# Selective-scan stage of a hybrid encoder layer on one Trainium2 core: which engine builds the mask G and the skip term, where filler matmuls stand, and where two sets of background weight sums run

## The chip, the cores and the metric

One NeuronCore of a Trainium2 chip runs the whole program. TensorE (PE) multiplies matrices, VectorE (DVE) and ScalarE (ACT) work on rows of up to 128 partitions, GpSimd (POOL) can do the same kind of element-wise work and issues DMAs, SyncE (SP) only issues DMAs. Each engine runs its own instructions strictly in order and waits on semaphores for the others. The metric is the device time of one execution in microseconds (us); lower is better.

## The reference

For 512 tokens of width 2048, in float32:

```python
h = rmsnorm(x, norm_w);  u = h @ w_in                 # z, x/B/C, dt fwd/bwd, q, kv, z_attn, two gates
xbc = silu(dwconv(xbc, conv_w, conv_b))               # x: 32 heads of 64; B, C: 4 groups of 128
y_fwd = ssd_scan(xs, dtf, a_f, bm, cm)                # chunks of 128 tokens
y_bwd = flip(ssd_scan(flip(xs), flip(dtb), a_b, flip(bm), flip(cm)))
y = y_fwd + y_bwd + d_skip[:, None] * xs              # the last term is the skip term
y = rmsnorm per group of (y * silu(z))
o = bidir_attention(...) * silu(z_attn)               # 16 heads, full softmax over 512 tokens
merged = sigmoid(g_ssm) * (y @ w_proj_ssm) + sigmoid(g_attn) * (o @ w_proj_attn)
out = rmsnorm(x + merged @ w_out, final_norm_w)
```

Inside one chunk `ssd_scan` needs, for every head, a 128 by 128 mask: decay(l, s) times (C_l . B_s) times dt_s. The kernel adds the forward mask (l not before s) and the backward one and multiplies by x once. That combined mask is the tile `G` below.

## The kernel before

Every float32 matmul is made of three matmuls of a faster 32-bit type: a weight is split by ACT into a rounded part `wh` (line 163 or 433) and by DVE into the rest `wl` (164 or 434), and PE adds wh\*x_h, wl\*x_h and wh\*x_l (lines 168 to 170, 578 to 580). The stages in order of time in the profile:

- 0 to 40 us: x is loaded, normalised and turned.
- 40 to 567 us: the dt columns, the x/B/C columns of group 0, and the gates z, g_ssm and g_attn by a Strassen scheme.
- 567 to about 1120 us: the scan, four groups of eight heads (`ssd_group`), which the change is about. PE's time is mostly filled with other products: the x/B/C columns of the next group, the q and kv columns, the z_attn columns. They are generators in a queue `fill`. The function `gap()` takes a fixed share of them, so that PE has something to do while the other engines prepare the next step.
- 1190 to about 1500 us: attention, head by head (`scores`, `trans`, `pv`), filled with the q/k/v products of later heads.
- 1500 us to the end: the projections of both branches and the output projection, by the Strassen scheme, whose weight sums T1 and T3 (`t_jobs`) have been formed in DRAM: for each, one DMA copies one weight block and a second DMA adds another to it (`accum_op`). There are 32 such DMAs for `wps` (the SSM projection) and 32 for `wpa` (the attention projection), all on POOL's queue. `wps` has them issued in the scan, one at every second `gap()`; `wpa` has them issued in attention, four per head in heads 0 to 7, each time after a tiny POOL product `pace` (line 1325) that waits for the head's softmax.

One group of the scan has three parts.

1. *Turning.* B and four tiles `xs` of x are turned by PE (line 942, four 128 by 128 transposes each, into the two banks of tag `pb`) and copied out by ACT (`b_h` line 947, `xT` line 953). In group 0, `dt_turn` and `dt_sums` come first: they turn dt and da and make the decay factors.
2. *State.* For three steps and two directions POOL weights x (`xw`, line 989), ACT and DVE split it (992, 993), PE forms the local state `loc`, DVE and ACT update and split the state, PE multiplies it by C (`off`), DVE scales it (1017) and POOL adds it to `yo` (1018). `yo` was set to the skip term by four POOL products per group (line 1022).
3. *Diagonal.* Four chunks c times two halves q of four heads. `cb_make` forms C.B on PE and masks it to `cbf` and `cbb` (DVE, 1043 and 1044). `seg_make` loads `da` (two broadcast DMAs on SP), DVE scans each (1056) and adds them to `E` (1059), ACT takes the exponential (1060), DVE multiplies `cbf` by the forward dt into `G` (1064), POOL multiplies `cbb` by the backward dt (1065), DVE adds (1066) and multiplies by E (1067). One gap later PE uses `G` (`diag`, line 1077); after the second half DVE and ACT gate and normalise y (`y_norm`).

PE's instructions stand in the order in which the code is written. The other engines' order is set by a planner with its own costs, except for the calls in `keep_in_program_order`. The order of the whole program ahead of the scan and behind attention is the same in both kernels.

The gap sizes of a group are set here (before the change):

```python
shares = [0.5 if g else 1.5, 1.1] + [0.8] * 6 + [1.25] * 10
left = [0, (10 * 48, 10 * 48, 9 * 48, 10 * 48)[g] / sum(shares)]
```

A unit of 48 is one product tile: 48 matmuls of 128 by 512.

Of the kernel before, what the change touches and what calls it, by code (L numbers as in the profile page):

```python
# [11 lines left out]
F32 = mybir.dt.float32  # L12
F32R = mybir.dt.float32r
I32 = mybir.dt.int32
AF = mybir.ActivationFunctionType
# [57 lines left out]
def build(tc, a):  # L73
# [231 lines left out]
    def dt_turn():  # L305
        tp = pb()
        dt64 = dt_t[0]
        for c in range(TT):
            pe.transpose(tp[:, c * P:(c + 1) * P], dt64[:, c * P:(c + 1) * P], ident)
        tpv = tp.rearrange("p (c k) -> p c k", c=TT)  # L310
        act.copy(dtT, tpv[:, :, 0:64])
        act.copy(daT, tpv[:, :, 64:128])

    def dt_sums():
        sm = pa()
        smv = sm.rearrange("p (k d c h) -> p k d c h", k=2, d=2, c=TT)
        for kk, dd, mask in ((0, 0, m_le), (0, 1, m_ge), (1, 0, m_gt), (1, 1, m_lt)):
            pe.matmul(smv[:, kk, dd], mask, daT[:, :, dd * NH:(dd + 1) * NH], start=True, stop=True)
        act.activation(ex.rearrange("p k d c h -> p (k d c h)"), sm, AF.Exp)
        tot = pb()  # L320
        pe.matmul(tot[:, 0:256], ones, daT.rearrange("p c h -> p (c h)"), start=True, stop=True)
        act.activation(dec.rearrange("p c h -> p (c h)"), tot[:, 0:256], AF.Exp)
        for dd in range(2):
            dve.tensor_mul(wst[:, dd], ex[:, 1, dd], dtT[:, :, dd * NH:(dd + 1) * NH])
# [152 lines left out]
    def t_jobs(w):  # L477

        jobs = []
        for cp in range(2):  # L480
            for name, kh, cb in (("T1", 0, 0), ("T3", 1, 1)):
                for m in range(4):
                    d = t_d[w, cp, name][:, m * 1024:(m + 1) * 1024]
                    i = 2 * len(jobs) // 2
                    jobs.append((lambda d=d, cp=cp, kh=kh, cb=cb, m=m: pool.dma_start(d, a[w][cp, kh, cb, m]),
                                 lambda d=d, cp=cp, m=m: pool.dma_start(d, a[w][cp, 0, 1, m], accum_op=ALU.add)))
        order = []
        for i in range(len(jobs) + 2):
            if i < len(jobs):
                order.append(jobs[i][0])  # L490
            if i >= 2:
                order.append(jobs[i - 2][1])
        return deque(order)

    background = t_jobs("wps")

    def in_background(n=1):
        for _ in range(n):
            if background:
                tc.keep_in_program_order(background.popleft()())  # L500
# [355 lines left out]
    def bc_heads(t, n):  # L856

        return t.unsqueeze(2).broadcast_to([P, t.shape[1], n])

    def flat(t):  # L860
        return t.rearrange("p h k -> p (h k)")
# [67 lines left out]
    def ssd_group(g):  # L929
# [15 lines left out]
        def post_b():  # L945
            tp = transposed(BT)
            act.copy(flat(b_h), tp)
            dve.tensor_sub(flat(b_l), tp, flat(b_h).bitcast(F32))

        def post_x(ct, xs):  # L950
            def f():
                tp = transposed(xs)
                act.copy(xT[:, :, ct * P:(ct + 1) * P], tp.rearrange("p (c k) -> p c k", c=TT))
            return f
# [6 lines left out]
                fill.add(("xbc", g + 1) if i == 5 else "xbc", xbc_gen(g + 1, i, tmp2))  # L961
        for kind, n in ((("qkv", 4),), (("qkv", 4),), (("qkv", 2), ("za", 1)), (("za", 10),))[g]:
            add_fill(kind, n)
        shares = [0.5 if g else 1.5, 1.1] + [0.8] * 6 + [1.25] * 10
        left = [0, (10 * 48, 10 * 48, 9 * 48, 10 * 48)[g] / sum(shares)]

        def gap():
            if len(shares) % 2:
                in_background()
            left[0] += shares.pop(0) * left[1]  # L970
            left[0] -= fill.run(left[0])

        gap()
        if g == 0:
            dt_turn()
            dt_sums()
        post_b()
        for ct in range(4):
            post_x(ct, xss[ct])()
        gap()  # L980

# [14 lines left out]
        def state(dd, c, xw):  # L996
            loc = pa("loc")
            mm3(loc, b_h[:, c, :], b_l[:, c, :], xw[0], xw[1], True, True)
            if S[dd] is None:
                S[dd] = sw.tile([P, HPG, 64], F32, tag=f"S{dd}", name=f"S{dd}")  # L1000
                dve.tensor_copy(flat(S[dd]), loc)
            else:
                s_ = S[dd]
                dve.tensor_mul(s_, s_, bc_heads(dec[:, c, dd * NH + g * HPG:dd * NH + (g + 1) * HPG], 64))
                dve.tensor_add(flat(s_), flat(s_), loc)
            s_h = sw.tile([P, SEQ], F32R, tag="r", bufs=6, name="s_h")
            s_l = sw.tile([P, SEQ], F32R, tag="r", bufs=6, name="s_l")
            act.copy(s_h, flat(S[dd]))
            dve.tensor_sub(s_l, flat(S[dd]), s_h.bitcast(F32))
            return s_h, s_l  # L1010
# [7 lines left out]
            pool.tensor_add(yo[:, c], yo[:, c], tmp)  # L1018

        nxt = [state_in(0, 0), state_in(1, 3)]  # L1020
        for c in range(TT):
            pool.tensor_mul(yoh[:, c], xTh[:, c], bc_heads(dsk[:, hs], 64))
        for i in range(3):
            ss = [state(0, i, nxt[0]), state(1, 3 - i, nxt[1])]
            if i < 2:
                nxt = [state_in(0, i + 1), state_in(1, 2 - i)]
            gap()
            if turns:
                y_turn(*turns.popleft())
            offdiag(0, i + 1, ss[0])  # L1030
            offdiag(1, 2 - i, ss[1])
            gap()
# [4 lines left out]
        def cb_make(c):  # L1037
# [6 lines left out]
            dve.tensor_mul(cbb, cb[:, 0:P], m_ge)  # L1044
            cbs[c] = (cbf, cbb)

        def seg_make(c, q):

            h0 = g * HPG + q * 4
            sums = []  # L1050
            for dd, mask in ((0, scan_f), (1, scan_b)):
                da = sw.tile([P, 4, P], F32, tag=f"da{dd}", bufs=2, name=f"da{dd}")
                src = da_d[dd * NH + h0:dd * NH + h0 + 4, c * P:(c + 1) * P]
                tc.keep_in_program_order(nc.sync.dma_start(da, src.unsqueeze(0).broadcast_to([P, 4, P])))
                sums.append(tmp2("sum"))
                dve.tensor_tensor_scan(sums[dd], flat(da), mask, 0.0, ALU.add, ALU.mult)  # L1056
            sf, sb = (t.rearrange("p (h l) -> p h l", h=4) for t in sums)
            E = sw.tile([P, 4, P], F32, tag="E", bufs=2, name="E")
            dve.tensor_add(E, sf, sb[:, :, ::-1])
            act.activation(flat(E), flat(E), AF.Exp)  # L1060
            G = sw.tile([P, 4, P], F32, tag="G", bufs=2, name="G")
            G2 = tmp2("G2").rearrange("p (h l) -> p h l", h=4)
            cbf, cbb = cbs[c]
            dve.tensor_mul(G, bc_heads(dtT[:, c, h0:h0 + 4], P), cbf.unsqueeze(1).broadcast_to([P, 4, P]))
            pool.tensor_mul(G2, bc_heads(dtT[:, c, NH + h0:NH + h0 + 4], P), cbb.unsqueeze(1).broadcast_to([P, 4, P]))
            dve.tensor_add(G, G, G2)
            dve.tensor_mul(G, G, E)
            return G

# [13 lines left out]
                turns.append((c, g, y))  # L1083

        last = None
        for c in range(TT):
            cb_make(c)
            for q in range(2):
                G = seg_make(c, q)
                if q == 1:  # L1090
                    zs[c] = z_load(c, g)
                gap()
                if q == 1 and len(turns) > 1:
                    y_turn(*turns.popleft())
                if last:
                    diag(*last)
                last = (c, q, G)
# [202 lines left out]
    fill.run(24)  # L1300

    heads = {}
    in_background(len(background))
    background.extend(t_jobs("wpa"))
    pace = few(1)

    def scores(hd, t):
        qh, ql, kh, kl, stack, zt = qks[hd]
        tk = slice(t * P, (t + 1) * P)
        s = pa("s")  # L1310
        pe.matmul(s, qh[:, tk], kh, start=True, stop=False)
        pe.matmul(s, qh[:, tk], kl, start=False, stop=False)
        pe.matmul(s, ql[:, tk], kh, start=False, stop=False)
        pe.matmul(s, stack[:, tk], kra, start=False, stop=False)
        pe.matmul(s, stack[:, tk], krb, start=False, stop=True)
        mx, nm, sm_ = (hi.tile([P, 1], F32, tag=n, bufs=4, name=n) for n in ("mx", "nm", "sm_"))
        dve.tensor_reduce(mx, s, AX.X, ALU.max)
        dve.tensor_scalar_mul(nm, mx, -SCALE)  # L1318
        pr = at_t("pr")
        act.activation(pr, s, AF.Exp, bias=nm, scale=SCALE, accum_out=sm_)  # L1320
        dve.reciprocal(sm_, sm_)
        dve.tensor_scalar_mul(pr, pr, sm_)
        heads[hd][2][t] = pr
        if background and t == 1:
            pool.tensor_mul(pace, sm_, sm_)
            in_background(4)

    def trans(hd, t):
        tk = slice(t * P, (t + 1) * P)
# [468 lines left out]
```

## Time and profile before

| | |
|---|---|
| median of 3 runs | 2020.08 us (2014.58 to 2021.41) |
| the profiled execution | 2014.14 us, of which the span below is 2012.4 us |
| PE, DVE, ACT, POOL busy over the span | 96%, 76%, 49%, 16% |
| scan stage, 565 to 1120 us: PE, DVE, ACT, POOL busy | 532.6, 462.8, 303.2, 174.2 of 555 us |

A busy PE counts a matmul as 0.39 us long, although in a steady stage a new one starts every 0.225 us (222 in 50 us), so the busy time hides 0.16 us at the start of each wait. The clock column in a table by stage is the share of full TensorE clock that was granted. Waits are named by the engine and line that ended them.

### The profile page before, as it was taken

Reading aid. Unit: us, or ns where it says so; the run is one execution under the profiler, and the core shown is the slowest. Engines: PE = TensorE matmul, PEld = TensorE weight load, DVE = VectorE, ACT = ScalarE, POOL = GpSimd, SP = SyncE. Lnnn points to the kernel's source line nnn. Section 1 sums busy time; section 2 is a strip of 40 time slices with the busy share of each in tenths; the row PEclk is TensorE's granted clock in tenths of the full one; section 3 lists DMA queues with packets and bytes.
Section 4 is the critical chain, followed back from the end, with each engine's and each line's share of the span. In section 5 each row is a group of like instructions: output and inputs, shape, how many; then the busy total and the mean of one; then the engine's idle time right before and its main releaser. Section 6 shows DMA issues by size and latency. Waiting matters only on the chain.

```text
span 2012.4 us, 24716 instructions
## 1 busy us (share of the span) xinstructions
PE 1940.6 (96%) x9026; PEld 1603.2 (80%) x9026; DVE 1520.6 (76%) x2000; ACT 985.2 (49%) x1370; POOL 323.2 (16%) x357
## 2 busy tenths in 40 slices
PE   6999999999999999999999999999999999999997
PEld 4888888888878778777788888887878787888886
DVE  7976676676659979899787577666676899879467
ACT  6444445444444655646546444444455555444343
POOL 0001001001023243152331011110011111100011
PEclk9999999999999999999999999999999999999999
DMA  5468558558446756776675857783278787847446
GB/s 192 162 191 213 147 136 220 146 131 224 127 157 166 222 164 194 243 214 205 182 199 157 240 163 201 204 221 112 75 205 299 221 290 286 286 157 247 158 90 161
DMA packets 168907, 382.78 MB, mean 190 GB/s; under 512 B 16272, under 2 KB 65552, under 8 KB 168592
## 3 DMA queue, kind: packets, MB, share of 16 engines
q1 hardware_dynamic: 103248, 233.61, 35.5%
q0 software_dynamic: 30656, 103.30, 23.5%
q10 hardware_dynamic: 34880, 44.28, 6.1%
q8 instruction: 71, 1.16, 0.2%
q14 instruction: 52, 0.43, 0.1%
HBM read 329.22 MB, written 98.04 MB: 212 GB/s over the span
## 4 chain that ended last, share of the span: by engine, by line
PE 70%; DVE 14%; DMA 7%; issue 5%; ACT 3%; POOL 1%; SPq 0%; DVEq 0%; POOLq 0%; ACTq 0%
PE P L579 11%; PE P L580 11%; PE P L578 11%; PE za L168 2%; PE za L169 2%; PE za L170 2%; DVE sum L1056 2%; PE xbc L168 2%; PE xbc L169 2%; PE xbc L170 2%; DVE wl L164 2%; PE f L1565 1%; PE f L1566 1%; PE f L1567 1%; DMA wraw<-wps 1%
## 5 line engine op out<-in xcount | busy, mean ns | idle before, releaser
L433 ACT CAST wh<-X 128x1024 fp32r<-128x1024 f32 x164 | 172.4, 1054 | 196.4 <-PE P L580 152.1
L434 DVE TENSOR_TENSOR wl<-X,wh 128x1024 fp32r<-128x1024 f32 x164 | 199.9, 1223 | 90.7 <-ACT wh L433 90.3
L164 DVE TENSOR_TENSOR wl<-wraw,wh 128x1024 fp32r<-128x1024 f32 (+2 forms) x148 | 176.6, 1194 | 83.6 <-ACT wh L163 83.1
L163 ACT CAST wh<-wraw 128x1024 fp32r<-128x1024 f32 (+2 forms) x150 | 145.0, 969 | 132.0 <-PE xbc L169 35.5
L434 DVE TENSOR_TENSOR wl<-Y,wh 128x1024 fp32r<-128x1024 f32 x88 | 107.6, 1224 | 70.3 <-ACT wh L433 70.3
L168 PE MATMUL xbc<-h_h,wh 128*128 128x512 f32 x384 | 151.8, 395 | 0.0
L433 ACT CAST wh<-Y 128x1024 fp32r<-128x1024 f32 x88 | 92.7, 1054 | 117.0 <-PE P L580 105.8
L170 PE MATMUL xbc<-h_h,wl 128*128 128x512 f32 x384 | 149.9, 390 | 0.0
L169 PE MATMUL xbc<-h_l,wh 128*128 128x512 f32 x384 | 149.7, 390 | 0.0
L578 PE MATMUL P<-wh,h_h 128*128 128x512 f32 x384 | 149.4, 389 | 0.0
L579 PE MATMUL P<-wl,h_h 128*128 128x512 f32 x384 | 149.4, 389 | 0.0
L580 PE MATMUL P<-wh,h_l 128*128 128x512 f32 x384 | 149.4, 389 | 0.0
L434 DVE TENSOR_TENSOR wl<-wraw,wh 128x1024 fp32r<-128x1024 f32 x68 | 83.2, 1223 | 63.7 <-ACT wh L433 63.7
L433 ACT CAST wh<-wraw 128x1024 fp32r<-128x1024 f32 x68 | 71.6, 1053 | 117.5 <-PE P L580 63.5
L579 PE MATMUL P<-wl,S 128*128 128x512 f32 x288 | 112.4, 390 | 0.5 <-DVE wl L434 0.3
L578 PE MATMUL P<-wh,S 128*128 128x512 f32 x288 | 112.1, 389 | 0.0
L580 PE MATMUL P<-wh,S 128*128 128x512 f32 x288 | 112.1, 389 | 0.0
L168 PE MATMUL za<-h_h,wh 128*128 128x512 f32 x256 | 101.1, 395 | 0.0
L170 PE MATMUL za<-h_h,wl 128*128 128x512 f32 x256 | 99.8, 390 | 0.0
L169 PE MATMUL za<-h_l,wh 128*128 128x512 f32 x256 | 99.6, 389 | 0.0
L1056 DVE TENSOR_TENSOR_SCAN sum<-da,scn 128x512 f32<-128x512 f32 x64 | 86.3, 1362 | 0.0
L1320 ACT ACTIVATE pr<-s,nm 128x512 f32<-128x512 f32 x64 | 44.1, 690 | 83.6 <-DVE nm L1318 82.8
(743 smaller groups left out, 5213.9 us busy)
## 6 DMA issues: line engine op xcount, KB each, us to landing
wraw<-wi SPq DMA_DIRECT2D x102, 512.0 KB, 4.0
T_wps<-wps POOLq DMA_DIRECT2D x32, 512.0 KB, 6.2
da<-da_d SPq DMA_DIRECT2D x64, 256.0 KB, 4.5
T_wpa<-wpa POOLq DMA_DIRECT2D x32, 512.0 KB, 9.5
wraw<-wps SPq DMA_DIRECT2D x24, 512.0 KB, 5.6
wraw<-wo SPq DMA_DIRECT2D x20, 512.0 KB, 3.6
xbc_d<-xbc ACTq DMA_DIRECT2D x24, 256.0 KB, 3.1
wraw<-wun SPq DMA_DIRECT2D x16, 384.0 KB, 3.1
```

What stands on the lines that cost most here:

```text
L163: act.copy(h, raw)
L164: (dve if ahead[0] else pool).tensor_sub(l, raw, h.bitcast(F32))
L168: pe.matmul(out, wh, xh, start=start, stop=False)
L169: pe.matmul(out, wh, xl, start=False, stop=False)
L170: pe.matmul(out, wl, xh, start=False, stop=stop)
L433: i = act.copy(hi_, raw)
L434: dve.tensor_sub(lo_, raw, hi_.bitcast(F32))
L578: pe.matmul(bs[i], xh, wh, start=(j == 0), stop=False)
L579: pe.matmul(bs[i], xh, wl, start=False, stop=False)
L580: pe.matmul(bs[i], xl, wh, start=False, stop=(j == 7))
L1056: dve.tensor_tensor_scan(sums[dd], flat(da), mask, 0.0, ALU.add, ALU.mult)
L1320: act.activation(pr, s, AF.Exp, bias=nm, scale=SCALE, accum_out=sm_)
```

## The change

- The forward part of `G` is made by four ACT copies per half chunk, one for each head, with the head's dt as the per-partition scale; the backward part is multiplied and added by one DVE operation per head. The DVE product, the POOL product and the DVE sum over four heads go.
- The skip term is set by eight ACT copies per group (one per head, over all four chunks, 128 by 4 by 64) in place of four POOL products. In the program they stand after the first two local states.
- In the turning part six filler matmuls stand ahead of each x tile; group 0 also gets twelve behind `dt_turn` and nine behind `dt_sums`. They are taken from the group's total, and the first gap of group 0 has share 0.5, not 1.5.
- No background sum is issued in the scan. All 64 are issued in attention: four per head in heads 0 to 7, six per head from head 8 on.
- The two `da` loads of a half chunk are issued one half chunk earlier.

```diff
     background = t_jobs("wps")
+    background.extend(t_jobs("wpa"))
...
-        shares = [0.5 if g else 1.5, 1.1] + [0.8] * 6 + [1.25] * 10
-        left = [0, (10 * 48, 10 * 48, 9 * 48, 10 * 48)[g] / sum(shares)]
+        shares = [0.5, 1.1] + [0.8] * 6 + [1.25] * 10
+        left = [0, ((10 * 48 - 21, 10 * 48, 9 * 48, 10 * 48)[g] - 24) / sum(shares)]
 
         def gap():
-            if len(shares) % 2:
-                in_background()
             left[0] += shares.pop(0) * left[1]
             left[0] -= fill.run(left[0])
+
+        def bit(n):
+            left[0] += n - fill.run(n)
 
         gap()
         if g == 0:
             dt_turn()
+            bit(12)
             dt_sums()
+            bit(9)
         post_b()
         for ct in range(4):
+            bit(6)
             post_x(ct, xss[ct])()
         gap()
...
-        for c in range(TT):
-            pool.tensor_mul(yoh[:, c], xTh[:, c], bc_heads(dsk[:, hs], 64))
         for i in range(3):
             ss = [state(0, i, nxt[0]), state(1, 3 - i, nxt[1])]
+            if i == 0:
+                for j in range(HPG):
+                    act.activation(yoh[:, :, j], xTh[:, :, j], AF.Copy, scale=dsk[:, g * HPG + j:g * HPG + j + 1])
...
+        das = deque()
+
+        def da_load(c, q):
...
-            G2 = tmp2("G2").rearrange("p (h l) -> p h l", h=4)
             cbf, cbb = cbs[c]
-            dve.tensor_mul(G, bc_heads(dtT[:, c, h0:h0 + 4], P), cbf.unsqueeze(1).broadcast_to([P, 4, P]))
-            pool.tensor_mul(G2, bc_heads(dtT[:, c, NH + h0:NH + h0 + 4], P), cbb.unsqueeze(1).broadcast_to([P, 4, P]))
-            dve.tensor_add(G, G, G2)
+            for j in range(4):
+                df, db = (dtT[:, c, o + h0 + j:o + h0 + j + 1] for o in (0, NH))
+                act.activation(G[:, j], cbf, AF.Copy, scale=df)
+                dve.scalar_tensor_tensor(G[:, j], cbb, db, G[:, j], ALU.mult, ALU.add)
             dve.tensor_mul(G, G, E)
...
+        da_load(0, 0)
         for c in range(TT):
             cb_make(c)
             for q in range(2):
                 G = seg_make(c, q)
+                if (c, q) != (TT - 1, 1):
+                    da_load(c + q, 1 - q)
...
-    in_background(len(background))
-    background.extend(t_jobs("wpa"))
...
-            in_background(4)
+            in_background(4 if hd < 8 else 6)
```

Where the planner puts the new instructions is seen in the order of the built programs. On PE, at the turning of B and x in group 1, before the change (`pb` is the bank, `cst` holds the identity; `xbc` is the filler):

```order
L170 MATMUL xbc<-h_h,wl 128x512
L942 MATMUL pb<-cst,BT 128x128 x4
L942 MATMUL pb<-cst,xs 128x128 x16
L168 MATMUL xbc<-h_h,wh 128x512
L169 MATMUL xbc<-h_l,wh 128x512
```

All four tiles stood in one row of sixteen transposes. With the change, around the first of them:

```order
L943 MATMUL pb<-cst,BT 128x128 x4
L168 MATMUL xbc<-h_h,wh 128x512
L169 MATMUL xbc<-h_l,wh 128x512
L170 MATMUL xbc<-h_h,wl 128x512
L168 MATMUL xbc<-h_h,wh 128x512
L169 MATMUL xbc<-h_l,wh 128x512
L170 MATMUL xbc<-h_h,wl 128x512
L943 MATMUL pb<-cst,xs 128x128 x4
```

Six filler matmuls now lie ahead of each tile's four transposes.

On ACT, at the same place in the change (`yo` is the new skip term, `xT` the copies out of the banks, `xw_h` the first step of the state part):

```order
L954 COPY xT<-pb 128x4x128
L1030 ACTIVATE yo<-xT,dsk 128x4x64 x3
L954 COPY xT<-pb 128x4x128
L1030 ACTIVATE yo<-xT,dsk 128x4x64 x3
L954 COPY xT<-pb 128x4x128
L1030 ACTIVATE yo<-xT,dsk 128x4x64 x2
L163 CAST wh<-wraw 128x1024
L388 ACTIVATE cacc<-xbc,vec 128x512
L997 CAST xw_h<-xw 128x512 x2
```

The planner has moved the skip copies up from behind the first states to between the second, third and fourth x copies.

On DVE, in the diagonal part of group 2 (second chunk), before and with the change:

```order
L1064 TENSOR_TENSOR G<-dtT,cbf 128x512
L1059 TENSOR_TENSOR E<-sum 128x512
L1066 TENSOR_TENSOR G<-G,G_7259 128x512
L164 TENSOR_TENSOR wl<-wraw,wh 128x1024
L1056 SCALAR_TENSOR_TENSOR sum<-da_7318,scn 128x512
```

```order
L1073 TENSOR_TENSOR E<-sum 128x512
L1049 TENSOR_TENSOR cbf<-cb,cst 128x128
L1050 TENSOR_TENSOR cbb<-cb,cst 128x128
L1080 SCALAR_TENSOR_TENSOR G<-cbb,dtT,G 128x128 x4
L1081 TENSOR_TENSOR G<-G,E 128x512
L164 TENSOR_TENSOR wl<-wraw,wh 128x1024
```

The four operations on G stand directly behind the masks here, and between the masks and them ACT has to make its four copies.

More of the change, by code (lines that the diff above doesn't have):

```diff
@@ L1045, in cb_make @@
             cbs[c] = (cbf, cbb)
+        das = deque()
+        def da_load(c, q):
+            h0 = g * HPG + q * 4
+            das.append([])
+            for dd in range(2):
+                da = sw.tile([P, 4, P], F32, tag=f"da{dd}", bufs=2, name=f"da{dd}")
+                src = da_d[dd * NH + h0:dd * NH + h0 + 4, c * P:(c + 1) * P]
+                tc.keep_in_program_order(nc.sync.dma_start(da, src.unsqueeze(0).broadcast_to([P, 4, P])))
+                das[-1].append(da)
         def seg_make(c, q):
@@ L1050, in seg_make @@
             sums = []
[L1051 to L1054, printed above, removed]
+            for da, mask in zip(das.popleft(), (scan_f, scan_b)):
                 sums.append(tmp2("sum"))
-                dve.tensor_tensor_scan(sums[dd], flat(da), mask, 0.0, ALU.add, ALU.mult)
+                dve.tensor_tensor_scan(sums[-1], flat(da), mask, 0.0, ALU.add, ALU.mult)
             sf, sb = (t.rearrange("p (h l) -> p h l", h=4) for t in sums)
```

## The prediction

> **What bounds the kernel now.** I read the page's first part, then the table by stage, PE's waits in the scan, the chain of waits there, and the groups of DVE, ACT and POOL.
>
> ```profile
> span 2012.4 us, 24716 instructions
> PE 1940.6 (96%) x9026; PEld 1603.2 (80%) x9026; DVE 1520.6 (76%) x2000; ACT 985.2 (49%) x1370; POOL 323.2 (16%) x357
> ```
>
> PE sets the end; only PE's waits can be won. The table by stage shows those of the scan (columns: stage, length, busy us and count of PE, weight loads, DVE, ACT, POOL; granted clock, DMA share, GB/s):
>
> ```profile
> 576.00:594.00 18.00, 13.35 (x68) 9.86 (x67) 7.12 (x10) 9.23 (x16) 11.74 (x10) 0.95 0.50 179
> 594.00:626.00 32.00, 31.83 (x137) 25.91 (x136) 27.93 (x36) 13.78 (x20) 9.05 (x9) 0.97 0.42 132
> 626.00:694.00 68.00, 64.84 (x312) 53.41 (x311) 65.25 (x89) 38.56 (x51) 22.65 (x18) 1.00 0.71 197
> ...
> 757.00:828.00 71.00, 69.75 (x341) 58.30 (x339) 69.24 (x95) 42.13 (x55) 22.46 (x18) 1.00 0.69 201
> 893.00:962.00 69.00, 65.05 (x304) 53.79 (x303) 65.73 (x95) 37.54 (x52) 23.03 (x18) 0.95 0.74 222
> 1027.00:1094.00 67.00, 67.00 (x327) 56.31 (x326) 63.03 (x84) 36.92 (x49) 17.52 (x12) 1.00 0.63 181
> ```
>
> The first two are the turning and the states of group 0, the four long ones the diagonal parts. In those DVE is busy 94 to 98% of the time. PE is idle 3.2 us, 1.3 us and 4.0 us in the first three. In 893 to 962 the clock was 0.95 besides. What PE waited for in the scan (us in total, times, longest):
>
> ```profile
> PE pb L942 <- ACT xT L953: 5.7, 8, 1.5
> PE qkv L170 <- DVE wl L164: 3.3, 3, 1.2
> PE yb L1077 <- DVE G L1067: 2.9, 1, 2.9
> ...
> PE loc L168 <- ACT xbc L392: 2.1, 1, 2.1
> PE yb L1077 <- DVE y L1080: 2.0, 3, 0.9
> PE loc L168 <- ACT xw_h L992: 2.0, 1, 2.0
> PE pb L942 <- DVE b_l L948: 1.9, 2, 1.0
> PE loc L169 <- DVE xw_l L993: 1.1, 3, 0.5
> PE pa L318 <- ACT daT L312: 0.7, 1, 0.7
> PE off L169 <- DVE s_l L1009: 0.4, 2, 0.2
> PE pb L942 <- ACT dec L322: 0.2, 1, 0.2
> ```
>
> Three families. Turning: 5.7 + 1.9 + 0.7 + 0.2 = 8.5 us in 12 waits. First state: 2.1 + 2.0 + 1.1 + 0.4 = 5.6 in 7. Diagonal: 3.3 + 2.9 + 2.0 = 8.2 in 7. Each wait costs 0.16 us more than its idle time, since a busy matmul counts 0.39 us and a new one starts every 0.225 us (page group and stage row):
>
> ```profile
> L170 PE MATMUL xbc<-h_h,wl 128*128 128x512 f32 x384 | 149.9, 390 | 0.0
> 300.00:350.00 50.00, 50.00 (x222) 41.40 (x221) 30.54 (x31) 25.06 (x28) 6.84 (x8) 1.00 0.89 227
> ```
>
> So the families cost 10.4, 6.7 and 9.3 us. The missing clock adds 18 x 0.05 + 32 x 0.03 = 1.9 us in group 0, right behind the waits for `loc`, and 69 x 0.05 = 3.4 us in group 2, behind the 2.9 us wait. In all about 32 us, 1.6% of the time: the change cannot win more in the scan.
>
> **The change part by part.**
>
> *Turning.* Two banks hold the turned tiles, so the third tile waits for ACT's copy of the first.
>
> ```profile
> L953 ACT COPY xT<-pb 128x512 f32<-128x512 f32 x16 | 9.1, 585 | 5.9 <-PE pb L942 5.9
> ```
>
> A copy takes 0.585 us; the six matmuls now ahead of a tile take 6 x 0.225 = 1.35. This covers the copy twice. But the planner has put skip copies between the x copies. Their price, 128x256 with a pointer scale, lies between two rows with such a scale, 0.366 for 128x128 and 0.722 for 128x512; a third of the way is 0.49, and I take 0.50 us.
>
> ```profile
> L905 ACT ACTIVATE y<-turn,vec 128x128 f32<-128x128 f32 x32 | 9.5, 366 | 1.4 <-PE turn L902 1.4
> L896 ACT ACTIVATE y<-y,rr 128x512 f32<-128x512 f32 x16 | 11.5, 722 | 13.5 <-DVE rr L191 12.3 <-ACT y L905 1.0
> ```
>
> Three skip copies and an x copy, 2.1 us, stand against 1.35 plus four transposes (about 0.45) on PE: ACT falls 0.3 us behind per tile, but PE needs a bank only two tiles later. In group 0 `daT` now stands behind the issue of the `dsk` load on ACT's queue and may cost 1 us. I leave 2.5 us: **gain 8**, bounds 4 and 10. The 21 and 24 matmuls are taken from other gaps, 1.6 per diagonal gap (0.4 us of cover).
>
> *First state.* POOL made the four skip products ahead of the first `xw`:
>
> ```profile
> L1022 POOL TENSOR_TENSOR yo<-xT,dsk 128x512 f32<-128x512 f32 x16 | 23.3, 1487 | 5.7 <-ACT xT L953 5.7
> L989 POOL TENSOR_TENSOR xw<-xT,wst 128x512 f32<-128x512 f32 x24 | 31.5, 1333 | 65.3 <-ACT xT L953 38.5 <-DVE rt L190 26.7
> ```
>
> That is 4 x 1.49 = 6 us off the path xT, xw, xw_h, loc. Back come the skip copies ahead of the last xT (6 x 0.50 = 3, partly hidden by the longer turning) and two behind it. The net is 2 to 4 us earlier, the longest waits are 2.1: **gain 5** of 6.7, bounds 2 and 6.7.
>
> *Diagonal, DVE.* Per half chunk go 0.802 + 0.883 = 1.69 us of DVE (lines 1064, 1066). Four operations of 128x128 come. The nearest row is the mask, 0.28; the row with a pointer scalar (0.735 for 510 elements) is no longer than those of line 1064 without one, so it adds little, 0.05 at most:
>
> ```profile
> L1064 DVE TENSOR_TENSOR G<-dtT,cbf 128x512 f32<-128x512 f32 x32 | 25.5, 802 | 0.0
> L1066 DVE TENSOR_TENSOR G<-G,G 128x512 f32<-128x512 f32 x32 | 28.3, 883 | 2.9 <-POOL G L1065 2.8
> L1043 DVE TENSOR_TENSOR cbf<-cb,cst 128x128 f32<-128x128 f32 x16 | 4.5, 280 | 2.4 <-PE cb L1040 2.4
> L389 DVE SCALAR_TENSOR_TENSOR cacc<-xbc,vec,cacc 128x510 f32<-128x510 f32 x18 | 13.2, 735 | 0.3 <-ACT cacc L388 0.3
> ```
>
> 1.12 to 1.32 us against 1.69: 0.4 to 0.6 us less, 3 to 4.6 us per diagonal part. POOL's products go too, and DVE runs longer while POOL works: this sum took 1.52 us beside a POOL product, where the mean of its group is 0.88 (DVE's row, then POOL's, of 640 to 651):
>
> ```profile
> 649.98 1.52 DVE L1066 TENSOR_TENSOR G<-G,G 128x512 f32<-128x512 f32 x1 [0.94 <-POOL G L1065]
> 648.59 2.35 POOL L1065 TENSOR_TENSOR G<-dtT,cbb 128x512 f32<-128x512 f32 x2 [12.63 <-DVE cbb L1044]
> ```
>
> The scans, mean 1.362 and least 1.193, lose up to 64 x 0.17 = 11 us to this in all; I take half back, 1.4 us per part.
>
> ```profile
> L1056 DVE TENSOR_TENSOR_SCAN sum<-da,scn 128x512 f32<-128x512 f32 x64 | 86.3, 1362 | 0.0
> L1056 DVE TENSOR_TENSOR_SCAN sum<-da,scn x64: 1193/1212/2245, 626.3 to 1086.4; 128x512 f32<-128x512 f32 x64
> ```
>
> Together DVE falls from 65 to about 60 of 68 us. [...]
>
> Against the saving stands a new wait: DVE's first piece needs ACT's first copy of G, which needs `cbf`. Where the pieces stand right behind the masks, DVE waits at least one ACT copy, about 0.5 us, with `wl` and the scans behind it, and PE behind `wl`. With one such place per chunk, 16 x 0.5 to 1.5 us = 2 to 6 us per part, it takes back half of DVE's room or all of it. **Gain 5** of 9.3, bounds 0 and 9.3.
>
> *Clock.* If the waits that preceded the losses go, they go: all 1.9 of group 0, 2 of the 3.4 of group 2. **Gain 4**, bounds 0 and 5.3.
>
> *`da` ahead.* No wait of DVE on a `da` load is in its groups (idle 0.0 before the scans): nothing.
>
> *Sums.* The 32 `wps` DMAs leave the scan; there PE does not wait on loads, so 0. In attention, heads 8 to 13 get 32 more.
>
> ```profile
> 1200.00:1350.00 150.00, 148.67 (x787) 125.33 (x786) 105.30 (x213) 66.89 (x136) 25.33 (x43) 1.00 0.77 202
> 1350.00:1450.00 100.00, 96.94 (x513) 81.60 (x512) 66.58 (x134) 44.48 (x87) 0.81 (x1) 1.00 0.40 108
> 1500.00:1560.00 60.00, 57.35 (x266) 46.89 (x264) 39.17 (x57) 30.89 (x44) 11.18 (x19) 1.00 0.89 295
> ```
>
> Heads 0 to 7 carry the same load with PE idle 0.9%; the lighter stage behind has 3.1%, so load is not what PE waits for there. At worst its 120 us go to the 4.4% of 1500 to 1560: 1.6 us. I take **a loss of 1**. On POOL's queue they stand ahead of sums of `o` that wait for head 11 anyway.
>
> Sum: 8 + 5 + 5 + 4 - 1 = 21, from 2014.1 (span 2012.4, 1.7 around it) to 1993. The median, 2020.1, lies 5.9 above this execution, the lowest run 0.4. I add 2 for that: **1995 us**.
>
> **The rivals.**
>
> *A: DVE stays the pace of the diagonal.* The in-order waits on ACT eat what DVE saves, and the cover taken by the tiles is missing. For it: the order of the pieces. Against: group 3, whose DVE is busy 94%, has no idle PE. Turning and state win 13 and 1.9 of clock, minus 1: 2000, with the 2 for the median 2002.
>
> *B: ACT becomes the pace, and the kernel is slower.* Each part gets 32 copies of 128x128. Price, by the 128x128 row above, which reads PSUM, and a little more for SBUF: 0.40 us.
>
> ```profile
> L894 ACT ACTIVATE z<-y 128x512 f32<-128x512 f32 x16 | 10.1, 629 | 20.7 <-DVE y L892 20.6
> L1060 ACT ACTIVATE E<-E 128x512 f32<-128x512 f32 x32 | 20.2, 632 | 54.3 <-DVE E L1059 54.2
> ```
>
> ACT would be busy 38.6 + 12.8 = 51.4 of 68 us. It also waits: for E 54.3, and 20.7 and 13.5 for y (rows above), 22 us per part. If none of it shrinks or is filled by the copies, ACT needs 73.5 us per part, 5.5 too many, 22 in all, as `wh` comes late: 2000 + 22 + 2 = 2024, and beyond with more. It decides once busy time and waits together pass 68. Against: the waits come from a late DVE, and the copies mostly stand ahead of the exponential, in this very gap. [...]
>
> *C: weights late in heads 8 to 13.* 3 us per head where a load lands after its turn, 18 in all: 1993 + 18 + 2 = 2013. Against: the rows of heads 0 to 7.
>
> **How the numbers follow.** Forecast 0.60 (its own range 1984 to 2004), A 0.20, C 0.10, B 0.10. The range: everything won is 2014 - 32 = 1982, and a little more; above, A and most of C: 1980 to 2012. What a measurement tells from no change is 0.3%, 6 us: faster is below 2014. Forecast and A are (0.80), C half (0.05), less 0.03 for a forecast that misses by much: 0.82. Slower 0.07 from B and 0.01 more; same 0.10.
>
> **What would show it.** Right: the waits of `pb` for xT and of `loc` nearly gone; DVE near 60 us in each diagonal part, ACT about 51; POOL about half as busy in the scan; full clock at group 2; heads 8 to 13 at about 0.8 DMA share and 3% idle PE. Wrong: PE waiting for `wl` behind `wh` more than before (B), DVE idle before line 1080 by more than 5 us per part with PE's waits for G still there (A), waits for `wraw` in attention (C).

## The result, and the profile after

| | before | after |
|---|---|---|
| median | 2018.92 us (2014.58 to 2022.2, 8 runs) | 2007.89 us (1999.77 to 2013.03, 8 runs) |
| profiled execution | 2014.14 us, span 2012.4 | 2010.63 us, span 2008.8 |

The ratio after to before is 0.9943, 95% interval 0.9929 to 0.9956: 11.5 us faster (9 to 14). 25 us were forecast. The profiled execution of after lies 2.7 us above its median and that of before 4.8 below, so the two traces differ by less than the runs.

The page of after, first part:

```profile
PE 1941.0 (97%) x9026; PEld 1606.9 (80%) x9026; DVE 1481.6 (74%) x2064; ACT 1032.3 (51%) x1527; POOL 250.1 (12%) x315
```

DVE has 39 us less, POOL 73 less and ACT 47 more, as the edits intend. The end of the scan is the last product with G. The view of that one line gives first and last start; before, then after:

```profile
L1077 PE MATMUL yb<-xT,G x256: 217/275/472, 642.5 to 1111.0; 128*128 128x64 f32 x128
```

```profile
L1091 PE MATMUL yb<-xT,G x256: 217/275/323, 641.3 to 1091.9; 128*128 128x64 f32 x128
```

**The scan ends 19.1 us earlier, where 22 were forecast.** So the missing part was not lost there. The table by stage of after, for the four diagonal parts (each from its first scan, for the same length as before):

```profile
624.00:692.00 68.00, 68.00 (x336) 57.29 (x335) 62.48 (x117) 48.66 (x87) 3.22 (x2) 1.00 0.60 186
753.00:824.00 71.00, 71.00 (x350) 59.77 (x349) 66.11 (x118) 53.86 (x95) 4.54 (x3) 1.00 0.59 185
886.00:955.00 69.00, 66.01 (x322) 54.42 (x321) 61.42 (x117) 51.60 (x93) 0.33 (x1) 1.00 0.56 172
1009.00:1076.00 67.00, 65.16 (x317) 54.16 (x316) 58.52 (x107) 50.39 (x85) 2.64 (x2) 1.00 0.56 165
```

In the four parts DVE fell from 263.3 to 248.5 us in all (62 a part; about 60 were forecast), ACT rose from 155.2 to 204.5, and the clock of group 2 is full. PE's waits in the whole scan:

```profile
PE pb L943 <- ACT dec L322: 2.0, 1, 2.0
PE za L170 <- DVE wl L164: 2.0, 2, 1.0
PE yb L1091 <- DVE G L1081: 1.7, 2, 0.9
PE loc L169 <- DVE xw_l L998: 1.4, 3, 0.8
PE yb L1091 <- DVE y L1094: 0.9, 1, 0.9
PE off L169 <- DVE s_l L1014: 0.7, 1, 0.7
PE qkv L170 <- DVE wl L164: 0.3, 1, 0.3
```

In all 9.0 us stand where 22.3 stood. The waits of `pb` for xT and of `loc` for xw_h are gone; of the 2.0 us behind `dec` (the decay factors, made by ACT in group 0) 0.2 stood before.

Behind the scan the picture turns: there the profiled execution of after takes 15.5 us longer than that of before (19.1 less the 3.6 between their spans). Three stages of after, two of attention and the start of the projections, then the second of them before:

```profile
1350.00:1450.00 100.00, 97.58 (x509) 82.13 (x510) 65.52 (x134) 42.02 (x85) 21.03 (x35) 1.00 0.80 218
1450.00:1500.00 50.00, 40.00 (x184) 32.22 (x182) 29.66 (x57) 21.73 (x40) 8.72 (x11) 0.93 0.99 251
1500.00:1560.00 60.00, 56.18 (x248) 45.97 (x249) 39.73 (x55) 31.65 (x43) 10.74 (x18) 0.96 0.87 290
```

```profile
1450.00:1500.00 50.00, 47.36 (x224) 38.33 (x225) 33.74 (x68) 22.65 (x44) 6.03 (x7) 1.00 0.64 161
```

Heads 8 to 11 carry the sums at a DMA share of 0.80 without harm. In 1450 to 1500, heads 12 and 13, the share is 0.99 where it was 0.64, PE is busy 7.4 us less, and the clock is short by 3.5 us there and 2.4 in the next stage. The chain of waits of after names the link (start, length, what):

```profile
1469.49 5.34 DMA wraw<-wps
1474.93 1.06 ACT wh L433
1476.02 1.23 DVE wl L434
...
1479.55 0.57 DVE pr L1337
...
1486.60 10.73 DMA wraw<-wps
...
1500.27 0.49 DVE pr L1337
```

The weights of the SSM projection land late; in the chain `wh` (1.06 us) and `wl` (1.23 us) follow the load, the softmax product `pr` comes behind both, and PE, idle for 3.68 us by then, behind `pr`. This happens twice, behind the load at 1469 and behind that at 1487. In PE's waits of 1440 to 1600 this is one row, after and then before:

```profile
PE pb L1348 <- DVE pr L1337: 10.0, 2, 6.3
```

```profile
PE pb L1333 <- DVE pr L1322: 3.7, 3, 1.5
```

The DMA view of after, 1440 to 1500 (KB each, median us from issue to landing), then that of before for the same work, 1450 to 1510 (`xraw` is y, read back as the operand of the projection):

```profile
T_wpa<-wpa POOLq DMA_DIRECT2D x8, 512.0 KB, 10.9
wraw<-wps SPq DMA_DIRECT2D x6, 512.0 KB, 7.9
xraw<-yn_x SPq DMA_DIRECT2D x4, 512.0 KB, 8.5
```

```profile
wraw<-wps SPq DMA_DIRECT2D x7, 512.0 KB, 4.9
xraw<-yn_x SPq DMA_DIRECT2D x4, 512.0 KB, 5.3
```

Eight sums, six of head 12 and two of head 13, lie in this stretch, and these loads beside them take 1.6 times as long (7.9 and 8.5 us against 4.9 and 5.3). The theory that follows: the scan won about 19 us, and the sums in heads 12 and 13 gave back at least 8 of it (19.1 less the 11.5 that the runs differ by; the two traces alone would say 15).

### The profile page after: what moved, and what is told of

The parts are those of the page before. It is cut to its first block, busy times and chain, and to the rows that moved or that the text cites. A ratio compares the mean times of both kernels' runs of the same rounds, so it can differ in the third digit from the quotient of the medians.

```text
span 2008.8 us, 24843 instructions
## 1 busy us (share of the span) xinstructions
PE 1941.0 (97%) x9026; PEld 1606.9 (80%) x9026; DVE 1481.6 (74%) x2064; ACT 1032.3 (51%) x1527; POOL 250.1 (12%) x315
## 4 chain that ended last, share of the span: by engine, by line
PE 75%; DVE 10%; DMA 8%; issue 3%; ACT 3%; POOL 0%; SPq 0%; ACTq 0%; DVEq 0%; POOLq 0%
PE P L580 11%; PE P L581 11%; PE P L579 11%; PE xbc L168 3%; PE xbc L169 3%; PE xbc L170 3%; DMA wraw<-wps 2%; PE za L170 2%; PE za L168 2%; PE za L169 2%; PE qkv L168 1%; PE qkv L170 1%; PE qkv L169 1%; PE f L1582 1%; PE f L1581 1%
## 5 line engine op out<-in xcount | busy, mean ns | idle before, releaser
L170 PEld LDWEIGHTS xbc<-h_h,wl 128*128 128x128 f32 x384 | 72.3, 188 | 15.6
```

Source lines behind the costliest of these rows:

```text
L170: pe.matmul(out, wl, xh, start=False, stop=stop)
```

## The experiments

Ratios are to the kernel before, with 95% intervals; 0.001 is 2.0 us.

**Only the sums moved.** In the kernel before, not the changed one:

```diff
     background = t_jobs("wps")
+    background.extend(t_jobs("wpa"))
...
-            if len(shares) % 2:
-                in_background()
...
-    in_background(len(background))
-    background.extend(t_jobs("wpa"))
...
-            in_background(4)
+            in_background(4 if hd < 8 else 6)
```

> The kernel before with one edit: all 64 sums in attention as in the change (four per head in heads 0 to 7, six from head 8 on). Theory: slower than before by 10 to 13 us, 2029 to 2033, ratio 1.005 to 1.0065, with PE waiting for the softmax near head 12. Rival (the sums cost nothing, as the prediction had it, 1 us): 2017 to 2022.

2030.02 us, ratio 1.0053 (1.0038 to 1.0067): 10.7 us slower. PE's waits for the same stage:

```profile
PE pb L1330 <- DVE pr L1319: 9.8, 2, 5.9
```

The same wait in the old kernel, with no other edit: the loss belongs to the moved sums.

**Earlier sums in attention.** In the changed kernel, six per head from the start (done in head 10), or five and then six (done in head 11):

```diff
-            in_background(4 if hd < 8 else 6)
+            in_background(6)
```

> The changed kernel with six sums per head from head 0 on, so that the last is issued at head 10 and not at head 13. Theory (it is the meeting of the sums with the load of weights and operands of the projections in heads 12 and 13 that costs): 1997 to 2002 us. Rival (any sum in attention costs, wherever it stands): 2006 to 2010; a DMA share near 1 in heads 0 to 7 with waits for weights there would speak for it.

```diff
-            in_background(4 if hd < 8 else 6)
+            in_background(5 if hd < 8 else 6)
```

> The changed kernel with five sums per head in heads 0 to 7 and six in heads 8 to 11, so that all 64 are issued by head 11. Theory (only the meeting with the loads of heads 12 and 13 costs): 1997 to 2001 us, as with six per head or 1 to 3 us better, since the DMA share in heads 0 to 7 falls from 0.95 to about 0.87. If the sums must be out of the way by head 10: 2002 to 2006.

Six: 2000.93 us, ratio 0.9897 (0.9878 to 0.9916). Five: 1996.43 us, ratio 0.9902 (0.9882 to 0.9921). The two can't be told apart; both are about 20 us faster than before and 8 to 9 faster than the change. With five per head the scan ends where it did (the last product with G starts at 1091.8), its trace is 12.3 us shorter behind that point than that of after (904.6 against 916.9 us), and the stage of heads 12 and 13 and the landing of its weights are whole again:

```profile
1200.00:1350.00 150.00, 146.61 (x788) 124.20 (x787) 103.20 (x208) 65.42 (x133) 28.01 (x46) 1.00 0.88 235
...
1450.00:1500.00 50.00, 46.70 (x223) 37.64 (x222) 37.11 (x73) 27.28 (x49) 9.88 (x15) 1.00 0.84 223
```

```profile
wraw<-wps SPq DMA_DIRECT2D x8, 512.0 KB, 4.9
```

The same 64 sums cost little while a head's loads leave room (share 0.88, PE idle 2% in heads 0 to 7) and 8 us where two more streams of loads begin. These versions beat both kernels.

**The sums back in the scan.** Was moving them needed at all? The changed kernel, with the sums where they were:

```diff
-    background.extend(t_jobs("wpa"))
...
         def gap():
+            if len(shares) % 2:
+                in_background()
...
     heads = {}
+    in_background(len(background))
+    background.extend(t_jobs("wpa"))
...
-            in_background(4 if hd < 8 else 6)
+            in_background(4)
```

> The changed kernel, but the sums of wps are issued in the scan again and the sums of wpa in heads 0 to 7 alone, four per head. Theory (the scan won 19 us by the trace, and the sums moved into heads 8 to 13 gave about 12 of it back through late weights): 1996 to 2000 us, ratio to before 0.988 to 0.991, the DMA share between heads 8 and 13 back near 0.4 to 0.6, and the long waits for the softmax in head 12 and 13 gone. Rival (what is lost behind the scan comes from the scan's earlier end, so that loads of the next stage collide): no faster than the change, 2005 to 2010.

2016.59 us, ratio 0.9989 (0.9974 to 1.0004). That is slower than either had it. The theory's attention part held, since PE is busy 46.8 of 50 us in 1450 to 1500; the scan's part did not: the last product with G starts at 1112.5, and the whole gain of the scan is gone: PE waits 22.3 us in the scan where it waited 9.0 in after. POOL's timeline shows one reason. Before the change, in group 0, and then in this run, in group 1:

```profile
648.59 2.35 POOL L1065 TENSOR_TENSOR G<-dtT,cbb 128x512 f32<-128x512 f32 x2 [12.63 <-DVE cbb L1044]
650.89 0.83 POOL L486 DMA_DIRECT2D T_wps<-wps  x1
```

```profile
758.90 0.57 POOL L485 DMA_DIRECT2D T_wps<-wps  x1
...
761.07 1.16 POOL L485 DMA_DIRECT2D T_wps<-wps  x1
```

Before the change POOL's products on G stood between two sums and waited for the masks of their half chunk (12.63 us here), so they also paced the sums. With those products gone the sums leave in one bunch, five in 3 us here. At 890 to 918, where seven left within the first 10 us, the DMA share is 1.00, a `da` load takes 12.5 us at the median and 17.7 at the longest, and DVE waits for it (the DMA view of the stretch, then DVE's waits in the scan):

```profile
da<-da_d SPq DMA_DIRECT2D x6, 256.0 KB, 12.5
```

```profile
DVE sum L1071 <- DMA da<-da_d: 12.6, 6, 3.1
```

**The bunch, or the sums?** The kernel above, with a pace of the kind that attention has:

```diff
         das = deque()
+        ssz2 = few(1)
...
                 G = seg_make(c, q)
+                if len(shares) % 2:
+                    tc.keep_in_program_order(pool.tensor_mul(ssz2, G[:, 0, 0:1], G[:, 0, 0:1]))
```

> The run sums_in_scan with one addition: a tiny POOL product on the finished G ahead of each sum of the diagonal part, so that a sum is issued only when the half chunk's G is done. In sums_in_scan POOL, which had lost its products on G, issued up to eight sums in 2 to 8 us (628 to 630, 759 to 764, 892 to 899), and in the last of these stretches a load of da took 17.7 us to land. Theory P (the bunches cost, not the sums): the scan ends near 1093 as in the change, no wait of DVE for da, 1995 to 2000 us, ratio 0.988 to 0.990. Rival (any sum in the changed scan costs, since its spare DMA time is gone): 2008 to 2017.

2015.14 us, ratio 0.9984 (0.9966 to 1.0002), in the rival's range. Theory P fell: no wait of DVE for `da` is left, but the scan ends at 1107.4. DVE's waits in the scan, then PE's:

```profile
DVE y L1096 <- DMA yn_x<-y: 10.1, 4, 6.2
```

```profile
PE yb L1093 <- DVE y L1096: 4.1, 1, 4.1
```

The stores of y now land too late for the two buffers of y (6.3 us at the median in 620 to 1092, 4.4 in after), and of the clock 6.9 us are missing in the scan against 1.7 in after (one less the granted clock, times 10 us, added over stages of 10 us from 560 to the scan's end; so below). What the bunching adds on top can't be told from two intervals that overlap.

**The fourth corner.** The kernel before, edited as in the first experiment, but with the rates of five per head:

```diff
-            in_background(4)
+            in_background(5 if hd < 8 else 6)
```

> The kernel before with one edit: all 64 sums in attention, five per head in heads 0 to 7 and six in heads 8 to 11. It fills the fourth corner of a square: old scan with the sums in it 2019, new scan with the sums in it 2014 to 2016, new scan with the sums in attention by head 11 1996. Theory I (the new scan and the moved sums win only together, since in the old scan DVE is the pace and a transfer that lands later is hidden): 2016 to 2022, the scan ending at 1108 to 1113. Rival (each wins by itself and the sums cost the old scan too): 2008 to 2013, the scan ending at 1100 to 1105.

2019.03 us, ratio 1.0002 (0.9991 to 1.0014), in the range of theory I. The square is full:

| ratio to before | sums of `wps` in the scan | sums in attention, done by head 11 |
|---|---|---|
| old scan | 1 | 1.0002 (0.9991 to 1.0014) |
| new scan | 0.9989 (0.9974 to 1.0004) | 0.9902 (0.9882 to 0.9921) |

Neither edit alone wins anything clear of the noise; together they win 20 us. The old scan ends at 1111.0 with the sums and at 1111.6 without. In these two traces that is a net result: without the sums PE waits 2.4 us less in it (19.9 against 22.3), and 3.4 us more of the clock are lost (8.5 against 5.1). Why the old scan bears the sums isn't shown: that DVE, as the pace, hides a late transfer is the expectation's argument.

**The parts of the new scan**, each undone alone in the changed kernel.

*G as before*, on DVE and POOL:

```diff
-            for j in range(4):
-                df, db = ...
-                act.activation(G[:, j], cbf, AF.Copy, scale=df)
-                dve.scalar_tensor_tensor(G[:, j], cbb, db, G[:, j], ALU.mult, ALU.add)
+            G2 = tmp2("G2").rearrange("p (h l) -> p h l", h=4)
+            dve.tensor_mul(G, bc_heads(dtT[:, c, h0:h0 + 4], P), ...)
+            pool.tensor_mul(G2, bc_heads(dtT[:, c, NH + h0:NH + h0 + 4], P), ...)
+            dve.tensor_add(G, G, G2)
```

> The changed kernel with G made as before (two products and a sum over four heads, one of the products on POOL). By the prediction the diagonal part gains 5 us from the new way and 2 of the clock with it: 2013 to 2016. If the 19 us of the scan come mostly from the new G: 2018 to 2022. If they come from the other edits: within 3 us of the change.

2019.57 us, ratio 1.0000 (0.9986 to 1.0013), in the second of the three ranges: undone alone, the new G is worth 11.5 us. The scan ends at 1102.9, with these waits in its diagonal, and 5 us more of lost clock than in after:

```profile
PE yb L1091 <- DVE y L1094: 7.2, 4, 3.2
PE yb L1091 <- DVE G L1081: 4.3, 1, 4.3
```

*Skip term on POOL*, ahead of the first local states:

```diff
         nxt = [state_in(0, 0), state_in(1, 3)]
+        for c in range(TT):
+            pool.tensor_mul(yoh[:, c], xTh[:, c], bc_heads(dsk[:, hs], 64))
...
-            if i == 0:
-                for j in range(HPG):
-                    act.activation(yoh[:, :, j], xTh[:, :, j], AF.Copy, ...)
```

> The changed kernel with the skip term made by four POOL products per group as before, ahead of the first states. The prediction gave the first state 5 us and a part of the clock: 2011 to 2015, with PE waiting for loc by xw_h again (2 to 5 us in all). If the filler in the turning already covers it: 2007 to 2010.

2019.46 us, ratio 0.9999 (0.9987 to 1.0012): worth 11.3 us, more than either range had it. The scan ends at 1103.4. PE waits for the first state again, and 5 us more of the clock are lost:

```profile
PE loc L168 <- ACT xw_h L997: 4.3, 2, 2.3
```

*No filler in the turning*: the calls of `bit` taken out, shares and totals as before the change.

```diff
-            bit(6)
             post_x(ct, xss[ct])()
```

> The changed kernel without the filler matmuls in the turning part (all gaps as before the change). The prediction gave the turning 8 us, of which the trace shows the waits of the banks for xT gone (5.7 us idle and more): expected 6 to 9 us slower than the change, 2014 to 2017. If the gain of the turning came from the missing POOL products and not from the filler: within 2 us of the change.

2012.25 us, ratio 0.9965 (0.9951 to 0.998): worth 4.4 us, between the two ranges. All of the turning's waits are back, and those of the diagonal in the list of after (4.9 us for `za`, `yb` and `qkv`) are nearly gone, 0.2 for `qkv` and 0.2 for `yb`:

```profile
PE pb L943 <- ACT xT L954: 5.8, 7, 1.5
PE pb L943 <- DVE b_l L949: 1.8, 2, 1.0
```

*`da` not fetched ahead*:

```diff
-        da_load(0, 0)
         for c in range(TT):
             cb_make(c)
             for q in range(2):
+                da_load(c, q)
                 G = seg_make(c, q)
-                if (c, q) != (TT - 1, 1):
-                    da_load(c + q, 1 - q)
```

> The changed kernel with the two da loads issued in the half chunk that uses them, as before the change. The prediction gave the earlier fetch nothing: 2006 to 2010, within 2 us of the change. If the faster DVE needs the fetch ahead: DVE waits for da before its scans, and the time is 2012 to 2018.

2011.22 us, ratio 0.9949 (0.9929 to 0.997), the change's own (0.9943) within its interval: nothing that these runs can tell.

**Sums ahead of the scan.** The gates' stage seemed to have room:

```diff
             self.hook(cp, "P6")
+            if self.w in ("wz", "wgs", "wga"):
+                tc.keep_in_program_order(pool.tensor_mul(gate_pace, u[0][:, 0:1], u[1][:, 0:1]))
+                in_background(3)
```

and the same behind `self.hook(cp, "P7")`; the sums of `wpa` stay at four per head.

> The changed kernel with the sums of wps issued ahead of the scan, in the stage of the gates (135 to 567 us, PE without idle time, DMA share 0.44 to 0.55 in most of it): three behind the products P6 and P7 of each pair, each time after a tiny POOL product on the result; the sums of wpa as before the change, four per head in heads 0 to 7. Theory (the sums cost in the scan and in heads 8 to 13, for want of DMA time, and nowhere else): the gates stage ends at 567 us as before, the scan near 1092, attention as before the change: 1993 to 1998 us, ratio 0.987 to 0.989, the fastest of all. If they cost wherever they stand: 2000 us and more.

2014.16 us, ratio 0.9988 (0.9973 to 1.0004). The theory fell. PE's busy time in 135 to 567 us, and its waits there; after has 432.00 busy of 432 and no wait:

```profile
135.00:567.00 432.00, 424.02 (x1848) 345.19 (x1847) 282.59 (x276) 196.27 (x220) 67.26 (x87) 1.00 0.76 200
```

```profile
PE P L579 <- DVE wl L434: 4.8, 11, 0.8
PE P L578 <- ACT wh L433: 2.9, 2, 2.3
```

The gates end 13 us later (60 matmuls fewer stand in the stretch, at 0.225 us each 13.5), and the scan then ends at 1103.9. After's mean share of 0.63 in this stretch was no spare room for this: three sums at once put the split weights late 13 times, by up to 2.3 us. Single sums there weren't tried.

## Why the prediction was right or wrong

**The failed step is the term *Sums*.** It took "a loss of 1", at worst 1.6 us, in 1500 to 1560. The runs show 8 (the change against five or six per head) to 10.7 us (the sums moved alone). It went wrong in two places. The first is where it looked: it bounded the loss by the mean load of heads 0 to 7, which heads 8 to 11 did carry unharmed, and it left out the stage of 1450 to 1500 (its rows go from 1350 to 1450 on to 1500 to 1560), where the loads of `wps` and y begin. The share of 0.8 and the 3% of idle PE that it expected for heads 8 to 13 held to 1450; behind that the table reads 0.99 and 20%. The second is its sentence that the sums "stand ahead of sums of `o` that wait for head 11 anyway": this is about the queue, and the loss came from the DMA engines, whose share read 0.99 while the sums on one queue and the loads on another were under way. The loads on SP went from 4.9 to 7.9 us beside the sums on POOL.

**Its other half, "there PE does not wait on loads, so 0", was right for the scan it was read from and wrong for the scan it was meant for.** In the old scan the sums cost 0 (square, upper row); in the new one about 18 us (lower row). The prediction's parts were costed one by one against the trace of before, and this one became a condition for the others.

**Rival C was the right mechanism with the wrong extent.** Its sign, waits for `wraw` in attention, is there, in two heads and not six: 10.0 us idle in 2 waits where before had 3.7, and 5.9 of lost clock. Its price of 18 was about twice what the runs gave. With the measured loss in place of 1, the forecast's own sum is 2014 - 22 + 8 to 11 + 2, or 2002 to 2005; with the scan's measured 19 in place of 22 it is 2005 to 2008.

**A and B did not happen.** ACT's 204.5 us in the four parts are 51.1 each, as forecast (51.4), and its waits for E shrank from 54.3 to 23.2. The groups of after that bear on this, of ACT and then of DVE (busy, mean ns, idle before):

```profile
L1079 ACT ACTIVATE G<-cbf,dtT 128x128 f32<-128x128 f32 x128 | 42.5, 393 | 9.3 <-DVE cbf L1049 8.8 <-ACT G L1079 0.3
L1074 ACT ACTIVATE E<-E 128x512 f32<-128x512 f32 x32 | 20.3, 633 | 23.2 <-DVE E L1073 23.0
```

```profile
L1080 DVE SCALAR_TENSOR_TENSOR G<-cbb,dtT,G 128x128 f32<-128x128 f32 x128 | 40.1, 354 | 6.4 <-ACT G L1079 5.9
L1070 DVE TENSOR_TENSOR_SCAN sum<-da,scn 128x512 f32<-128x512 f32 x64 | 81.2, 1290 | 0.2
```

The prices held: 0.393 us for a G copy against 0.40 taken. A DVE piece took 0.354, more than the 0.28 to 0.33 taken, so four cost 1.42 against 1.69 and the saving is 0.27 us per half chunk, not 0.4 to 0.6. The scans, without POOL's products beside them, fell from 1.362 to 1.290 us, 4.6 us in all, where 5.6 were taken (1.374 in the old scan without the sums, where POOL's products stand). DVE's wait for ACT's copies, 2 to 6 us per part in the prediction, is 5.9 in the whole scan.

**The other terms held, read as the prediction meant them:** as PE's waits in the scan, each with 0.16 us more. In after the turning costs 2.2 us where it cost 10.4 (8.2 won, 8 forecast), the first state 2.7 where it cost 6.7 (4.0 won, 5 forecast), the diagonal 5.9 where it cost 9.3 (3.4 won, 5 forecast), and by the tables 1.7 us of the clock are lost in the scan where 5.1 were (3.4 won, 4 forecast). That is 19.0 in all, the 19.1 of the scan.

What a part is worth when it is undone alone is another quantity: turning 4.4, first state 11.3, G 11.5, `da` 0. These add to 27 where the scan won 19. They overlap, since each undone part also brings back lost clock of about 5 us (the turning's less, 2). The turning's is low because its filler was taken from the diagonal's gaps: the prediction gave that cover no price, and 4.9 us of waits stand there now, where 0.4 stand without the filler.

## What to carry to other kernels

Cost a background transfer at the stage where it will run after the change, in windows as short as the stages there, and look for the window in which another stream of loads begins; a stage's mean DMA share says little, here a stage with 0.63 had no room for sums in threes, and one with 0.80 carried them. An engine that loses its work may have been the brake on what stands behind it in its queue: ask what paced it. And where two edits may need each other, run the four corners: here each alone was worth nothing clear of the noise, and both together 20 us.

## What the hardware showed that was not expected

One wait cost more than its own length. After PE's idle 3.68 us at 1476 to 1480 matmuls start 0.43 us apart instead of 0.225 (rows of PE's timeline of after, behind the wait):

```profile
1480.25 1.09 PE L1348 MATMUL pb<-cst,pr 128*128 128x128 f32 x4 [3.68 <-DVE pr L1337]
...
1481.99 0.63 PE L1328 MATMUL s<-kh,ql 128*128 128x512 f32 x1
1482.42 0.63 PE L1329 MATMUL s<-kra,stack 128*128 128x512 f32 x1
```

The granted clock of 1479 to 1484 is 0.66, so 1.7 us are lost on top of the wait. Shorter waits don't show this so plainly: the 2.0 us wait for `dec` in after was followed by 1.7 us of lost clock, and the same wait, 2.3 us long in the kernel with the skip term on POOL, by none. What lowers the clock isn't shown.
